# Dropping rows past a capacity: the pass-through copy cut into 4 KB pieces on one queue, with hand-written semaphores and one branch

## Chip, cores and metric

The kernel runs on one core of one Trainium2 chip. The metric is the time of one execution in device microseconds. The kernel before takes 106.83 us, the median of three runs (107.74, 106.81, 106.83).

## What is computed

`x` is float32 of shape 16 x 1024 x 512 (16,384 rows of 2 KB, 33.55 MB), `token_positions` one integer per row, `capacity` the number 256.

```python
mask = token_positions < capacity
return (x * mask[..., np.newaxis]).astype(np.float32)
```

The positions are drawn from 0 to 255, so with this input no row is dropped, and the output is a copy of `x`. Both kernels still look at every position, and both have a path for dropped rows that multiplies by the mask. That path is not taken here.

## The kernel before

Both kernels begin by copying all of `x` to the output, from device memory to device memory, before the mask is known. Meanwhile the mask is computed, and a flag tells whether any row of a section is dropped. Only where the flag is 1 is the section loaded to on-chip memory, multiplied and stored again.

**The copy (lines 73 to 77).** The 16,384 rows are seen as 128 groups ("p") of 128 rows ("n"). Copy k of four takes rows 32k to 32k+31 of every group: 128 pieces of 64 KB, one every 256 KB. Copies 0 and 2 are issued on SP's DMA queue (`hw[0]`), copies 1 and 3 on ACT's. The outermost dimension has 128 entries, and the transfer is spread over the core's 16 DMA engines in blocks of 8 entries, so that one engine's pieces begin 2 MB from the next engine's.

**The mask (lines 55 to 134).** SP first loads the positions (128 KB, line 57) into 16 partitions of 2,048 32-bit words. VectorE (DVE) converts the low and high words (L81, L82), makes four comparisons (L86 to L98) and joins them (L101 to L103). TensorE turns the 16 x 1024 result into 128 x 128 with eight selection matrices (L107), which GpSimd (POOL) has built (L60 to L65). DVE copies and sums it (L115, L118), TensorE adds the sums over partitions (L124), and DVE makes four flags of them (L126, L134). POOL also clears two 8 MB tiles (L153).

**The path for dropped rows (lines 136 to 197).** SP, ACT and DVE read four flags each. Four loads (L163) and four stores (L183) are conditional transfers: they are issued always, and move nothing where the flag is 0. The multiplications stand in an `If` on DVE. The order of waits is made by the framework: each store waits, among other things, for the copy of the same rows to have landed. SP and ACT thus stand at L183 until the copies are done.

Of the kernel before, what the change touches and what calls it, by code (L numbers as in the profile page):

```python
# [8 lines left out]
@with_exitstack  # L9
def kernel(  # L10
    ctx: ExitStack,
    tc: tile.TileContext,
    x: bass.AP,
    token_positions: bass.AP,
    capacity: bass.AP,
    out: bass.AP,
):
    nc = tc.nc
    P = nc.NUM_PARTITIONS
    fp32 = mybir.dt.float32  # L20
    i32 = mybir.dt.int32

    x_f = x.flatten_outer_dims()
    out_f = out.flatten_outer_dims()
    N, D = x_f.shape
    assert N % P == 0
    n_per_p = N // P

    x_r = x_f.rearrange("(p n) d -> p n d", p=P)
    out_r = out_f.rearrange("(p n) d -> p n d", p=P)  # L30

    tp_f = token_positions.flatten_outer_dims()
    tp_r = tp_f.rearrange("b s -> (b s)") if len(tp_f.shape) == 2 else tp_f
    tp_i32 = tp_r.bitcast(mybir.dt.int32)
    QP = 16
    G = P // QP
    tp_pn = tp_i32.rearrange("(q w) -> q w", q=QP)

    cap = float(int(capacity))

    FIX_COLS = 32
    assert n_per_p % FIX_COLS == 0
    n_fix = n_per_p // FIX_COLS
    rows_per_fix = P * FIX_COLS

    sp = nc.sync
    act = nc.scalar
    hw = (sp, act)

    mask_pool = ctx.enter_context(tc.tile_pool(name="mask", bufs=1))  # L50
    psum_pool = ctx.enter_context(tc.tile_pool(name="psum", bufs=1, space=bass.MemoryType.PSUM))
    NBUF = 2
    io_pool = ctx.enter_context(tc.tile_pool(name="io", bufs=1))

    rows_q = N // QP
    tp_tile = mask_pool.tile([QP, rows_q * 2], i32)
    sp.dma_start(out=tp_tile, in_=tp_pn)

    e_iota = mask_pool.tile([QP, P], i32, name="e_iota")
    nc.gpsimd.iota(e_iota, pattern=[[1, P]], base=0, channel_multiplier=-G)  # L60
    e_iota_f = mask_pool.tile([QP, P], fp32, name="e_iota_f")
    nc.gpsimd.tensor_copy(out=e_iota_f, in_=e_iota)  # L62
    e_all = mask_pool.tile([QP, G, P], fp32, name="e_all")
    for b in range(G):
        nc.gpsimd.tensor_scalar(  # L65
            out=e_all[:, b, :],
            in0=e_iota_f,
            scalar1=float(b),
            scalar2=None,
            op0=mybir.AluOpType.is_equal,  # L70
        )

    for k in range(n_fix):
        c0 = k * FIX_COLS
        hw[k % 2].dma_start(
            out=out_r[:, c0 : c0 + FIX_COLS, :], in_=x_r[:, c0 : c0 + FIX_COLS, :]
        )

    lo = mask_pool.tile([QP, G, P], fp32)
    hi = mask_pool.tile([QP, G, P], fp32)  # L80
    nc.vector.tensor_copy(out=lo, in_=tp_tile[:, 0 : 2 * rows_q : 2])  # L81
    nc.vector.tensor_copy(out=hi, in_=tp_tile[:, 1 : 2 * rows_q : 2])  # L82

    f_tile = mask_pool.tile([QP, G, P], fp32)
    t_hi = mask_pool.tile([QP, G, P], fp32)
    nc.vector.tensor_scalar(  # L86
        out=t_hi, in0=hi, scalar1=0.0, scalar2=None, op0=mybir.AluOpType.is_equal
    )
    m2 = mask_pool.tile([QP, G, P], fp32)
    nc.vector.tensor_scalar(  # L90
        out=m2, in0=lo, scalar1=cap, scalar2=None, op0=mybir.AluOpType.is_lt
    )
    m3 = mask_pool.tile([QP, G, P], fp32)
    nc.vector.tensor_scalar(  # L94
        out=m3, in0=lo, scalar1=0.0, scalar2=None, op0=mybir.AluOpType.is_ge
    )
    t_neg = mask_pool.tile([QP, G, P], fp32)
    nc.vector.tensor_scalar(  # L98
        out=t_neg, in0=hi, scalar1=0.0, scalar2=None, op0=mybir.AluOpType.is_lt
    )  # L100
    nc.vector.tensor_tensor(out=f_tile, in0=t_hi, in1=m2, op=mybir.AluOpType.mult)  # L101
    nc.vector.tensor_tensor(out=f_tile, in0=f_tile, in1=m3, op=mybir.AluOpType.mult)  # L102
    nc.vector.tensor_tensor(out=f_tile, in0=f_tile, in1=t_neg, op=mybir.AluOpType.add)  # L103

    m_psum = psum_pool.tile([P, P], fp32, space=bass.MemoryType.PSUM, name="m_psum")
    for b in range(G):
        nc.tensor.matmul(  # L107
            out=m_psum,
            lhsT=e_all[:, b, :],
            rhs=f_tile[:, b, :],  # L110
            start=(b == 0),
            stop=(b == G - 1),
        )
    m_tile = mask_pool.tile([P, n_fix, FIX_COLS], fp32)
    nc.vector.tensor_copy(out=m_tile, in_=m_psum)  # L115

    red = mask_pool.tile([P, n_fix], fp32)
    nc.vector.tensor_reduce(  # L118
        out=red, in_=m_tile, axis=mybir.AxisListType.X, op=mybir.AluOpType.add
    )  # L120
    ones = mask_pool.tile([P, 1], fp32)
    nc.vector.memset(ones, 1.0)  # L122
    s_psum = psum_pool.tile([1, n_fix], fp32, space=bass.MemoryType.PSUM)
    nc.tensor.matmul(out=s_psum, lhsT=ones, rhs=red, start=True, stop=True)  # L124
    flag_f = mask_pool.tile([1, n_fix], fp32)
    nc.vector.tensor_scalar(  # L126
        out=flag_f,
        in0=s_psum,
        scalar1=float(rows_per_fix) - 0.5,
        scalar2=None,  # L130
        op0=mybir.AluOpType.is_lt,
    )
    flag_i = mask_pool.tile([1, n_fix], i32)
    nc.vector.tensor_copy(out=flag_i, in_=flag_f)  # L134

    sp_flags = [
        sp.value_load(flag_i[0:1, u : u + 1], min_val=0, max_val=1)
        for u in range(n_fix)
    ]
    act_flags = [  # L140
        act.value_load(flag_i[0:1, u : u + 1], min_val=0, max_val=1)
        for u in range(n_fix)
    ]
    ve_flags = [
        nc.vector.value_load(flag_i[0:1, u : u + 1], min_val=0, max_val=1)
        for u in range(n_fix)
    ]
    eng_flags = {sp: sp_flags, act: act_flags}

    xts = []  # L150
    for b in range(NBUF):
        zt = io_pool.tile([P, FIX_COLS, D], fp32, name=f"xt_z{b}")
        nc.gpsimd.memset(zt, 0.0)  # L153
        xts.append(zt)

    ld_eng = {0: sp, 1: sp, 2: act, 3: act}
    st_eng = {0: act, 1: sp, 2: sp, 3: act}

    def emit_load_and_mul(u):
        f0 = u * FIX_COLS  # L160
        xt = xts[u % NBUF]
        eng = ld_eng[u]
        eng.dma_start(  # L163
            out=xt,
            in_=x_r[:, f0 : f0 + FIX_COLS, :],
            cond=eng_flags[eng][u],
            cond_hint=False,
        )
        with tc.If(ve_flags[u]):
            for j in range(FIX_COLS):  # L170
                nc.vector.tensor_scalar(
                    out=xt[:, j, :],
                    in0=xt[:, j, :],
                    scalar1=m_tile[:, u, j : j + 1],
                    scalar2=None,
                    op0=mybir.AluOpType.mult,
                )

    def emit_store(u):
        f0 = u * FIX_COLS  # L180
        xt = xts[u % NBUF]
        eng = st_eng[u]
        eng.dma_start(  # L183
            out=out_r[:, f0 : f0 + FIX_COLS, :],
            in_=xt,
            cond=eng_flags[eng][u],
            cond_hint=False,
        )

    emit_load_and_mul(0)  # L190
    emit_load_and_mul(1)
    emit_store(0)
    emit_store(1)
    emit_load_and_mul(2)
    emit_load_and_mul(3)
    emit_store(2)
    emit_store(3)


# [1 line left out]
_INS = ['x', 'token_positions', 'capacity']  # L201
_OUTS = [((16, 1024, 512), 'float32')]
#: Inputs that are plain numbers.
_NUMBERS = {'capacity': 256}


# [26 lines left out]
```

## Time and profile before

| What | Value |
|---|---|
| Timed runs | 107.74, 106.81, 106.83 us |
| Span of the profiled execution, first to last instruction | 104.9 us |
| Own time of the profiled execution | not listed apart; the median is 1.9 us above the span |
| DMA moved | 33.69 MB in 609 packets |
| Busy: DVE / POOL / PE | 46.6 / 50.7 / 3.9 us |
| Last DVE instruction of the mask (L134) begins | 54.51 us |

The profile is of one execution. The page lists, for each engine, busy time and groups of instructions with their mean duration. "DMA share" is the mean busy share of the core's 16 DMA engines in a stretch, and GB/s what they moved; a copy from memory to memory counts its bytes once. A packet is counted in the slice in which it begins. "SPq" and "ACTq" are the instruction queues that issue transfers. The page's memory counter (67.24 MB read, 67.11 MB written) is twice the 33.6 MB that the packets moved, which is the sum over the copies and the conditional transfers as they are written down, moved or not.

### The profile page before, as it was taken

To read this page: it belongs to the slowest core of one execution; us is meant where nothing else is said; L and a number is where in the kernel's file an instruction comes from. 1 tells how busy PE (TensorE), PEld (TensorE's weight loads), DVE (VectorE), ACT (ScalarE), POOL (GpSimd) and SP (SyncE) were. 2 spreads that over 40 slices of the span, in tenths; PEclk is the share of its full clock that TensorE was granted. 3 is DMA by queue.
4 is the path that set the end of the run, shared out by engine and by line. 5 is a ranking of instruction groups with operands and counts; after the bars stand their busy time and mean duration, and the time that the engine had idled before them with its cause. 6 is when DMAs were issued, how large, how long until landed. Compare 5 with 4: busy or idle time off the path is not lost.

```text
span 104.9 us, 202 instructions
## 1 busy us (share of the span) xinstructions
PE 3.9 (4%) x18; PEld 3.6 (3%) x18; DVE 46.6 (44%) x14; POOL 50.7 (48%) x16
## 2 busy tenths in 40 slices
PE   0000000000000000000940000000000000000000
PEld 0000000000000000000920000000000000000000
DVE  0599999999999999998030000000000000000000
POOL 7999999999999999999600000000000000000000
DMA  9299999909999939999919999759999929999930
GB/s 375 100 375 400 400 400 375 400 25 400 400 400 375 300 125 400 400 400 375 375 50 400 400 400 403 225 175 400 400 400 375 325 100 400 400 400 375 300 125 0
DMA packets 609, 33.69 MB, mean 321 GB/s; under 512 B 80, under 2 KB 80, under 8 KB 80
## 3 DMA queue, kind: packets, MB, share of 16 engines
q1 hardware_dynamic: 320, 16.91, 48.5%
q10 hardware_dynamic: 288, 16.78, 47.4%
q14 instruction: 1, 0.01, 0.0%
HBM read 67.24 MB, written 67.11 MB: 1281 GB/s over the span
## 4 chain that ended last, share of the span: by engine, by line
DVE 44%; PE 4%; DMA 3%; issue 0%
DVE lo L81 24%; DVE m L90 14%; PE m_psum L107 4%; DMA tp_tile<-in_token_positions_dram 3%; DVE f_tile L103 1%; DVE f_tile L102 1%; DVE f_tile L101 1%; DVE m L94 1%; DVE t_neg L98 1%; DVE t_hi L86 1%; DVE hi L82 1%; DVE m_tile L115 0%; DVE red L118 0%; PE s_psum L124 0%; DVE flag_f L126 0%
## 5 line engine op out<-in xcount | busy, mean ns | idle before, releaser
L153 POOL MEMSET xt_z<- 128x16384 f32 x2 | 28.0, 14012 | 0.0
L81 DVE CAST lo<-tp_tile 16x1024 f32<-16x1024 int32 x1 | 25.1, 25121 | 2.9 <-DMA tp_tile<-in_token_positions_dram 2.9
L62 POOL CAST e_iota_f<-e_iota 16x128 f32<-16x128 int32 x1 | 14.3, 14328 | 0.0
L90 DVE TENSOR_SCALAR m<-lo 16x1024 f32<-16x1024 f32 x1 | 14.3, 14305 | 0.0
L65 POOL TENSOR_SCALAR e_all<-e_iota_f 16x128 f32<-16x128 f32 x8 | 8.1, 1023 | 0.3
L107 PE MATMUL m_psum<-f_tile,e_all 16*128 16x128 f32 x16 | 3.8, 424 | 49.6 <-DVE f_tile L103 49.6
L107 PEld LDWEIGHTS m_psum<-f_tile,e_all 16*128 16x128 f32 x16 | 3.5, 326 | 49.6 <-POOL e_all L65 49.6
L115 DVE COPY m_tile<-m_psum 128x128 f32<-128x128 f32 x1 | 0.3, 292 | 3.9 <-PE m_psum L107 3.9
L103 DVE TENSOR_TENSOR f_tile<-f_tile,t_neg 16x1024 f32<-16x1024 f32 x1 | 1.2, 1211 | 0.0
L102 DVE TENSOR_TENSOR f_tile<-f_tile,m 16x1024 f32<-16x1024 f32 x1 | 1.2, 1211 | 0.0
L101 DVE TENSOR_TENSOR f_tile<-t_hi,m 16x1024 f32<-16x1024 f32 x1 | 1.2, 1204 | 0.0
L82 DVE CAST hi<-tp_tile 16x1024 f32<-16x1024 int32 x1 | 0.8, 760 | 0.0
L86 DVE TENSOR_SCALAR t_hi<-hi 16x1024 f32<-16x1024 f32 x1 | 0.8, 759 | 0.0
L94 DVE TENSOR_SCALAR m<-lo 16x1024 f32<-16x1024 f32 x1 | 0.8, 759 | 0.0
L98 DVE TENSOR_SCALAR t_neg<-hi 16x1024 f32<-16x1024 f32 x1 | 0.8, 759 | 0.0
L122 DVE MEMSET ones<- 128x1 f32 x1 | 0.1, 59 | 0.8 <-PEq L214 0.8
L60 POOL IOTA e_iota<- 16x128 int32 x1 | 0.2, 224 | 0.4 <-POOLq L214 0.4
L118 DVE TENSOR_REDUCE red<-m_tile 128x4 f32<-128x128 f32 x1 | 0.3, 286 | 0.0
L126 DVE TENSOR_SCALAR flag_f<-s_psum 1x4 f32<-1x4 f32 x1 | 0.1, 148 | 0.3 <-PE s_psum L124 0.3
L124 PE MATMUL s_psum<-red,ones 128*1 128x4 f32 x2 | 0.2, 166 | 0.7 <-DVE red L118 0.7
L214 POOL MEMSET const-float32-0.0<- 128x1 f32 x1 | 0.1, 98 | 0.2 <-issue 0.2
L134 DVE CAST flag_i<-flag_f 1x4 int32<-1x4 f32 x1 | 0.2, 156 | 0.0
(4 smaller groups left out, 0.4 us busy)
## 6 DMA issues: line engine op xcount, KB each, us to landing
tp_tile<-in_token_positions_dram SPq DMA_DIRECT2D x1, 128.0 KB
out_dram<-in_x_dram ACTq DMA_DIRECT2D x2
out_dram<-in_x_dram SPq DMA_DIRECT2D x2
xt_z<-in_x_dram SPq DMA_DIRECT2D x2
out_dram<-xt_z ACTq DMA_DIRECT2D x2
xt_z<-in_x_dram ACTq DMA_DIRECT2D x2
out_dram<-xt_z SPq DMA_DIRECT2D x2
```

Source lines behind the costliest of these rows:

```text
L62: nc.gpsimd.tensor_copy(out=e_iota_f, in_=e_iota)
L65: nc.gpsimd.tensor_scalar(out=e_all[:, b, :], in0=e_iota_f, scalar1=float(b), scalar2=None, op0=mybir.AluOpType.is_equal,)
L81: nc.vector.tensor_copy(out=lo, in_=tp_tile[:, 0 : 2 * rows_q : 2])
L82: nc.vector.tensor_copy(out=hi, in_=tp_tile[:, 1 : 2 * rows_q : 2])
L86: nc.vector.tensor_scalar(out=t_hi, in0=hi, scalar1=0.0, scalar2=None, op0=mybir.AluOpType.is_equal)
L90: nc.vector.tensor_scalar(out=m2, in0=lo, scalar1=cap, scalar2=None, op0=mybir.AluOpType.is_lt)
L94: nc.vector.tensor_scalar(out=m3, in0=lo, scalar1=0.0, scalar2=None, op0=mybir.AluOpType.is_ge)
L101: nc.vector.tensor_tensor(out=f_tile, in0=t_hi, in1=m2, op=mybir.AluOpType.mult)
L102: nc.vector.tensor_tensor(out=f_tile, in0=f_tile, in1=m3, op=mybir.AluOpType.mult)
L103: nc.vector.tensor_tensor(out=f_tile, in0=f_tile, in1=t_neg, op=mybir.AluOpType.add)
L107: nc.tensor.matmul(out=m_psum, lhsT=e_all[:, b, :], rhs=f_tile[:, b, :], start=(b == 0), stop=(b == G - 1),)
L153: nc.gpsimd.memset(zt, 0.0)
```

## The change

The copy is written anew. It goes out as 17 transfers on SP's queue alone: two of 1 MB, then fifteen of 2 MB, in order of address. Within a transfer the outermost dimension is e = 16, one entry per DMA engine; its inner dimensions are k blocks at a step of 64 KB, and 4 KB in each. Engine e thus takes the e-th 4 KB of every 64 KB.

The positions are loaded on ACT's queue into 128 partitions of 256 words, so that the mask needs no transposition: four DVE operations on 128 x 128 elements, one sum along the row, one matmul over partitions and one comparison make a single flag. The conversions of the words, the selection matrices, the eight matmuls and POOL's two 8 MB clears are gone.

The path for dropped rows stands in one `If` on SP, ACT and DVE, with plain transfers of 4 MB in two buffers. All waits are written by hand with semaphores, inside one section which the framework does not order (`tc.tile_critical()`). SP ends by waiting for all 17 copies.

```diff
-    for k in range(n_fix):
-        c0 = k * FIX_COLS
-        hw[k % 2].dma_start(
-            out=out_r[:, c0 : c0 + FIX_COLS, :], in_=x_r[:, c0 : c0 + FIX_COLS, :]
-        )
+        def copy(eng, first, count, view, **sizes):
+            eng.dma_start(
+                out=out_b[first : first + count].rearrange(view, **sizes),
+                in_=x_b[first : first + count].rearrange(view, **sizes),
+            ).then_inc(s_copy, 16)
+        KB = 1024 // 4
+        MB = 1024 * KB
+        first = 0
+        for size in [MB, MB] + [2 * MB] * 15:
+            copy(sp, first, size, "(k e c) -> e k c", e=16, c=4 * KB)
+            first += size
+            n_copy += 1
-    sp.dma_start(out=tp_tile, in_=tp_pn)
+        act.dma_start(out=tp, in_=tp_i32.rearrange("(p w) -> p w", p=P)).then_inc(s_tp, 16)
-    nc.vector.tensor_copy(out=lo, in_=tp_tile[:, 0 : 2 * rows_q : 2])
-    nc.vector.tensor_copy(out=hi, in_=tp_tile[:, 1 : 2 * rows_q : 2])
...
+        ve.wait_ge(s_tp, 16)
+        ve.tensor_scalar(
+            out=ge, in0=lo, scalar1=0.0, scalar2=None, op0=Alu.is_ge
+        ).then_inc(s_ve, 1)
...
+        ve.tensor_scalar(
+            out=drop_i, in0=total, scalar1=float(N) - 0.5, scalar2=None, op0=Alu.is_lt
+        ).then_inc(s_ve, 1)
+        for e in (sp, act, ve):
+            e.wait_ge(s_ve, 7)
...
+        with nc.If(drop):
...
-        nc.gpsimd.memset(zt, 0.0)
-    sp_flags = [
-        sp.value_load(flag_i[0:1, u : u + 1], min_val=0, max_val=1)
-        for u in range(n_fix)
-    ]
...
-        eng.dma_start(
-            out=out_r[:, f0 : f0 + FIX_COLS, :],
-            in_=xt,
-            cond=eng_flags[eng][u],
-            cond_hint=False,
-        )
...
+        sp.wait_ge(s_copy, 16 * n_copy)
```

## The prediction

> **What bounds the kernel now.** I read the page's head and its 40 slices first, then its chain, then the windows of the DMA column, and last the waits of SP's queue.
>
> ```profile
> span 104.9 us, 202 instructions
> PE 3.9 (4%) x18; PEld 3.6 (3%) x18; DVE 46.6 (44%) x14; POOL 50.7 (48%) x16
> ...
> DVE  0599999999999999998030000000000000000000
> POOL 7999999999999999999600000000000000000000
> DMA  9299999909999939999919999759999929999930
> GB/s 375 100 375 400 400 400 375 400 25 400 400 400 375 300 125 400 400 400 375 375 50 400 400 400 403 225 175 400 400 400 375 325 100 400 400 400 375 300 125 0
> ```
>
> No compute engine works in the second half; only the DMA row goes on. Its dips look like pauses and are none. A packet is 64 KB, lasts longer than a slice (2.62 us), and is counted where it begins, so now and then a slice has no beginnings. In the packet records each engine's packets follow one another without a gap: 32 of 64 KB on each of 16 engines, the first beginning at 2.25 us and the last ending at 103.09, so 100.84 us, and 100.84 / 32 = 3.15 us each. The chain (DVE 44%, PE 4%) ends with the mask at 54.7 us, half the span: it does not carry the end. The waits of SP's queue do:
>
> ```profile
> SPq L137 <- DVE flag_i L134: 52.2, 1, 52.2
> SPq L183 <- DMA out_dram<-in_x_dram: 44.5, 2, 41.7
> ```
>
> The first wait is for the flags; the second begins after it and lasts until the copies have landed. So the copies end the kernel, and the mask has some 45 us to spare. Windows placed at the packets' own boundaries show the rate (columns: stretch, length, busy time of PE, PEld, DVE and POOL with counts, clock, DMA share, GB/s):
>
> ```profile
> 2.00:5.10 3.10, 0.00 (x0) 0.00 (x0) 1.33 (x1) 3.10 (x1) 1.00 0.98 359
> 5.10:8.00 2.90, 0.00 (x0) 0.00 (x0) 2.90 (x1) 2.90 (x1) 1.00 1.01 362
> 8.00:11.00 3.00, 0.00 (x0) 0.00 (x0) 3.00 (x1) 3.00 (x1) 1.00 0.99 350
> 11.00:14.00 3.00, 0.00 (x0) 0.00 (x0) 3.00 (x1) 3.00 (x1) 1.00 1.05 350
> 14.00:17.30 3.30, 0.00 (x0) 0.00 (x0) 3.30 (x1) 3.30 (x2) 1.00 1.03 318
> ```
> ```profile
> 2.20:11.00 8.80, 0.00 (x0) 0.00 (x0) 7.23 (x1) 8.80 (x1) 1.00 1.00 360
> 11.00:23.60 12.60, 0.00 (x0) 0.00 (x0) 12.60 (x1) 12.60 (x2) 1.00 1.02 333
> 23.60:48.80 25.20, 0.00 (x0) 0.00 (x0) 25.13 (x9) 25.12 (x7) 1.00 1.00 333
> 73.90:102.20 28.30, 0.00 (x0) 0.00 (x0) 0.00 (x0) 0.00 (x0) 1.00 1.00 333
> ```
>
> The DMA engines are always taken (share about 1.00), yet move 360 GB/s at first and 333 later, with DVE and POOL busy (23.6 to 48.8) or idle (73.9 on) alike. Compute does not slow the copy. Nor is it the speed of a DMA engine by itself: the shortest 64 KB packets last 2.42 us (27.1 GB/s per engine, 434 for 16), the mean one 3.14. What the packets wait for in the other 0.7 us is on the memory's side, shared by all; which addresses the 16 engines have in hand at one time may matter to it. That address pattern is what the change touches.
>
> **The change part by part.** The sum is made against the profiled span of 104.9 us: 2.25 head + 100.84 copy + 1.8 tail. The median lies 1.9 above it.
>
> Mask and flag. Gone are 46.6 us of DVE (L81 alone 25.1, L90 14.3), POOL's 50.7 us, and the eight matmuls at L107 (3.8). In their place come six DVE operations, none over 128 elements per partition; L118 and L115 have that size at 0.29 us, so about 1.5 us, and one matmul (L124: 0.2). The gain on the end is zero, because the copy covers both chains: the new flag should stand before 15 us, over 80 us ahead of the end. What SP does after the flag (a wait, one value, one branch) comes after its 17 issues and before its wait for the copies, under the same cover. Were the cover gone, the chain of a few us would be the price. Conditional transfers: eight instructions of 0.1 to 0.3 us on two queues, most of them at 57 to 59 us, under the copies; the last two, at 103.5, stand in the tail.
>
> Head. Before, ACT issued a copy at 0.74 and SP its positions at 0.74; the first packet of the positions (16 rows) began at 1.86, that of the copy (128 rows) at 2.25. So 112 rows more cost 0.39 us. The new first transfer is 16 x 16 = 256 rows: another 0.45 us. SP issues it about 0.1 us later, behind a section entry (a no-op and a branch). First packet at 2.25 + 0.45 + 0.1 = 2.8 us, a loss of 0.55. Ends: 0 (engines begin as soon as their own rows are there) and 1.3 (all of it twice as dear).
>
> Issue. SP's issues took 418 ns for 16 rows and 609 ns for 128, 1.7 ns per row. For 512 rows that makes 1.26 us, for 256 rows 0.83: 15 x 1.26 + 2 x 0.83 = 20.6 us for the whole copy. If all of 609 ns went by rows, 4.8 ns each, it is 2.4 us per 2 MB transfer and 8,192 x 4.8 = 39 us. A 2 MB transfer takes 5.8 to 6.3 us to move, so the queue stays ahead at either price: zero, covered by the transfer before it; the 1 MB first transfer (2.9 us) covers the second's issue too. The positions go out on ACT's queue, ahead of nothing there.
>
> One queue in place of two. Each engine now takes all its pieces from one list. At most, every one of the 16 joints between transfers waits for its last write; the trace shows 0.35 us between the last packet's semaphore write and the landing, so 16 x 0.35 = 5.6 us. At least zero: in the trace the 4-byte semaphore packets last 9 ns and the next 64 KB packet begins within 20 ns, but from the other queue. I take zero, the nearer row, and keep 5.6 for the range.
>
> 4 KB pieces. An engine now has 512 pieces where it had 32. The nearest row of small pieces is the load of the positions: 8 KB packets following one another every 307 ns, against 301 ns at 27.1 GB/s, so 6 ns each; the first ones in a row lasted 461 ns, 155 more. At 6 ns a 4 KB piece takes 151 + 6 = 157 ns, and 512 take 80 us: below the copy's time now, so the engines could run ahead of the memory, and the piece itself costs nothing. At 155 ns, unhidden each time, it is 306 ns and 157 us. I take the first, since packets in a row are the case at hand; but the row writes on-chip memory and not device memory, and the other end stays open as a rival.
>
> Rate of the memory. Bounds: 333 GB/s (nothing changes), 360 (the first three rounds, as long as all engines march in step), and above it 434 (shortest packets). The new pattern keeps the 16 engines inside one 64 KB block that moves on, where they were 2 MB apart. I take 355, between the first stretch's 360 and the 350 of the next two, as the state in which engines are close together is the nearest to it: 33.55 / 0.355 = 94.5 us. This is the term that decides, and the trace does not show the pattern.
>
> Here the Trainium skill, in "HBM Reference", section "Specifications (TRN2)", puts the bandwidth of a memory domain at about 716 GB/s. The rows above are read and written at once, 2 x 333 = 667 and 2 x 360 = 720, so this trace comes up to that figure and not past it. By it the copy's floor is an estimated 67.1 / 0.716 = 93.7 us, and the total 100.2.
>
> A rule against the change stands in "DMA: Bandwidth & Descriptors", "Latency and other measured facts": copies between memory tensors in rows of 16 KB reached 214 GB/s at best, and less at large power-of-two steps (207 at 512 KB, 164 at 2 MB). This trace, with rows of 64 KB at steps of 256 KB and 2 MB, shows 333. If shorter rows are what made those copies slow, the new one would take an estimated 33.55 / 0.214 = 157 us or more; if the steps were, it gains. No run so far tells which.
>
> Tail. The last landing is at 103.43, SP's queue is through at 103.67, the span ends at 104.9. Afterwards SP has one wait and the section's exit in place of two conditional transfers. I take the same 1.8 us, with 1.3 and 2.5 as ends.
>
> Sum: 2.8 + 94.5 + 1.8 = 99.1 us of span, and 99.1 + 1.9 = 101.0.
>
> **The rivals.**
> 1. The address pattern does not matter, and the copy runs at 333 GB/s: 2.8 + 100.8 + 1.8 + 1.9 = 107.3. For it: the rate stays at 333 through all of the later stretches, whatever the other engines do. Against: the first three rounds at 360.
> 2. Slower: each 4 KB piece has a cost that the next does not hide. It decides from 100.84 / 512 = 197 ns a piece, 46 over the 151 of the bytes. At 60 over it is 211 x 512 = 108 us, in all 114.5; at the full 155, 157 us and 163. For it: 155 ns of start-up in the first packets, and 64 KB pieces that last 0.7 us longer than their bytes. Against: the 6 ns of packets in a row, and those 64 KB packets without any loss (2.42 us).
> 3. Joints on one queue: the forecast plus up to 5.6, 106.6. For it: 0.35 us to a landing; against: 9 ns packets.
> 4. The memory has more to give once the engines stand close: 157 ns a piece, 80 us, in all 86.9; halfway from 355 GB/s 94. Against: in no stretch do 16 engines together pass 362.
>
> **How the numbers follow.** Forecast 0.55, from 97 to 104 by the ends of head, tail and rate (360 to 345). Rival 1 0.11, rival 2 0.20, rival 3 0.06, rival 4 0.08. The range of 94 to 108 takes in the forecast, rivals 1 and 3 and half of rival 4, and leaves out rival 2 and the far half of 4. About 1% is what a measurement of this kernel can tell from no change. Faster by over 1% (below 105.8): the forecast, rival 4, and most of 3, 0.68. Within 1%: most of rival 1 and some of 3, 0.11. Slower: rival 2 and a part of 1, 0.21.
>
> **What would show it.** Copy stretches of a steady 350 to 360 GB/s confirm the rate; 333 says rival 1; a share of 1.00 at under 320 says rival 2; a share well under 1.00 says joints or issue. First packets before 3 us confirm the head; the last DVE instruction should end before 15 us; SP's last wait should be for the copies, and end 1 to 2 us before the span does. The prediction is wrong if the 4 KB packets last over 197 ns.

## The result, and the profile after

The changed kernel took 110.40, 110.69, 111.21 and 112.34 us, the kernel before beside it 106.81 to 107.74. The ratio is 1.034, with a 95% interval from 1.028 to 1.040: slower by about 3.4%, outside the predicted range of 94 to 108. (The 112.34 is left out of the ratio, as a disturbed run.) The profiled execution took 110.40 us over a span of 108.6, so 1.8 us lie around it.

The head of the page of the changed kernel, with its slices:

```profile
span 108.6 us, 90 instructions
PE 0.2 (0%) x2; PEld 0.1 (0%) x2; DVE 1.6 (1%) x7; POOL 0.2 (0%) x4
...
DVE  0500000000000000000000000000000000000000
DMA  2999999999999999999999999999998999999870
GB/s 71 338 305 273 389 305 339 299 299 380 279 383 264 345 327 278 342 320 330 344 312 329 276 385 288 330 338 309 353 294 326 344 344 329 302 356 312 339 308 24
DMA packets 8609, 33.69 MB, mean 310 GB/s; under 512 B 288, under 2 KB 416, under 8 KB 8608
```

The compute engines are all but gone, as the change set out: 46.6 us of DVE became 1.6, and the flag is there at 4.9 us. The DMA row shows no gap. Its rate now swings between 264 and 389 from slice to slice; with packets of 4 KB this is no artefact of counting.

The queue of SP, then the windows of the copy (columns as before):

```profile
SPq L151 <- DMA out_dram<-in_x_dram: 26.5, 1, 26.5
```
```profile
0.90 0.36 ACTq L85 DMA_DIRECT2D tp<-in_token_positions_dram  x1
0.95 79.03 SPq L69 DMA_DIRECT2D out_dram<-in_x_dram  x17
2.95 0.23 DVE L92 TENSOR_SCALAR ge<-tp 128x128 f32<-128x128 int32 x1 [1.88 <-DMA tp<-in_token_positions_dram]
```
```profile
2.50:15.10 12.60, 0.19 (x2) 0.09 (x2) 1.53 (x6) 0.00 (x0) 1.00 1.01 324
15.10:27.70 12.60, 0.00 (x0) 0.00 (x0) 0.00 (x0) 0.00 (x0) 1.00 1.03 323
27.70:52.90 25.20, 0.00 (x0) 0.00 (x0) 0.00 (x0) 0.00 (x0) 1.00 1.00 322
78.10:103.30 25.20, 0.00 (x0) 0.00 (x0) 0.00 (x0) 0.00 (x0) 1.00 0.99 329
103.30:107.00 3.70, 0.00 (x0) 0.00 (x0) 0.00 (x0) 0.00 (x0) 1.00 0.59 234
```

The wait for the copies still ends the kernel. The engines are as fully taken as before (about 1.00), at 322 to 329 GB/s, where the kernel before kept 333. In the last window the share falls to 0.59: some engines are done while others go on. By the packet records the copy begins at 2.48 us and ends at 106.95, 104.47 us against 100.84. So the whole loss (3.7 us of span) lies in the copy stretch (3.63); head and tail changed by +0.23 and -0.15 and cancel.

The packet records say more. The median 4 KB packet lasts 159 ns, the next one beginning 155 ns after it; the mean is 201. Nearly four fifths of the pieces (78%) last 165 ns or less, so they go at the engine's own speed; 9% last 300 to 1,835 ns. So an engine runs at full speed, then stands.

The 4-byte packets that end each transfer on its 16 engines show how far the engines part. In the kernel before, those of the copies lie within 0.6 to 1.0 us of one another. In the changed kernel they lie 1.0 us apart after the first transfer, 5.8 at most, and 2.5 at the last.

### The profile page after: what moved, and what is told of

Same layout as the page of the kernel before. It is cut to its first block, busy times and chain, and to the rows that moved or that the text cites. A ratio compares the mean times of both kernels' runs of the same rounds, so it can differ in the third digit from the quotient of the medians.

```text
span 108.6 us, 90 instructions
## 1 busy us (share of the span) xinstructions
PE 0.2 (0%) x2; PEld 0.1 (0%) x2; DVE 1.6 (1%) x7; POOL 0.2 (0%) x4
```

## The experiments

Two theories stood against one another at first. "Piece": each 4 KB piece has a cost that the next does not hide. "Queue": one queue, with its joints and its long issue, costs what a second would hide. A third, "closeness", was that 16 engines inside one 64 KB block collide. The chips of the runs differ by up to 2%, so only ratios to the kernel before on the same chip are compared. The packet records name neither the engine nor the address; distances between engines are those that the program writes down, with the entries of the outermost dimension taken to go to the 16 engines in order.

**1. The old copy in the new kernel.**

```diff
-        for size in [MB, MB] + [2 * MB] * 15:
-            copy(sp, first, size, "(k e c) -> e k c", e=16, c=4 * KB)
+        for k in range(4):
+            c0 = 32 * k
+            (sp, act)[k % 2].dma_start(
+                out=out_r[:, c0 : c0 + 32, :], in_=x_r[:, c0 : c0 + 32, :]
+            ).then_inc(s_copy, 16)
```

> The changed kernel with the copy of before: four transfers of 128 pieces of 64 KB on two queues. Everything else (mask, semaphores, branch) stays changed. If the loss lies in the copy alone, this takes 106 to 107 us, a copy stretch of some 100.8 us. If hand-written waits, section entry or exit cost something, it stays above 108.

It took 1.031 (1.026 to 1.037), and not for a reason that the theories named. Its timeline:

```profile
0.91 1.26 ACTq L79 DMA_DIRECT2D out_dram<-in_x_dram  x2
2.20 0.60 ACTq L85 DMA_DIRECT2D tp<-in_token_positions_dram  x1
106.98 0.23 DVE L92 TENSOR_SCALAR ge<-tp 128x128 f32<-128x128 int32 x1 [105.91 <-DMA tp<-in_token_positions_dram]
108.79 0.15 DVE L114 TENSOR_SCALAR drop_i<-total 1x1 int32<-1x1 f32 x1 [0.28 <-PE total L112]
```

The edit put ACT's two copies ahead of the positions in the same queue, so the positions landed with the copies, at 106.9 us, and the mask came after everything. The cover that the prediction relied on was gone, and the chain of a few us was the price. The edit was at fault, and the run says nothing of the copy.

**5. The same with the positions issued first** (the line of L85 moved above the loop).

> As the run with the old copy, but the positions are issued on ACT's queue ahead of ACT's two copies, so that they do not stand behind 16 MB. If the loss of the changed kernel lies in the copy's piece size alone, this ties with the kernel before (ratio 0.995 to 1.005). If section entry, exit or hand-written waits cost something, 1.01 or more.

Measured: 1.002 (0.999 to 1.005). Mask, hand-written waits, section and branch cost nothing and bring nothing that can be measured. The change's loss is the copy's.

**2 to 4. One property of the copy at a time.** Run 2 puts `c=64 * KB` for `c=4 * KB`; run 4 puts `(sp, act)[n_copy % 2]` for `sp`; run 3 moves the engines apart:

```diff
+        x_v = x_b.rearrange("(e k t c) -> t e k c", e=16, t=16, c=4 * KB)
+        out_v = out_b.rearrange("(e k t c) -> t e k c", e=16, t=16, c=4 * KB)
+        for t, k0, k1 in [(0, 0, 16), (0, 16, 32)] + [(t, 0, 32) for t in range(1, 16)]:
+            sp.dma_start(out=out_v[t][:, k0:k1, :], in_=x_v[t][:, k0:k1, :]).then_inc(s_copy, 16)
```

> The changed kernel with 64 KB in place of 4 KB: engine e takes the e-th 64 KB of every 1 MB, still 17 transfers on one queue. Theory 'piece' (each 4 KB piece has a cost of its own): 106 to 107 us, packets of 3.1 us. Theory 'closeness' (16 engines within one 64 KB block collide in memory): also near 107, since they now stand 64 KB apart. Theory 'one queue': stays at 110 to 111.

> The changed kernel with 4 KB pieces at steps of 64 KB as before, but each engine in its own 2 MB section: 2 MB apart, not 4 KB. Sizes and number of transfers, queue and pieces per engine are those of the changed kernel. Theory 'piece': 110 to 111 us again, mean piece 201 ns. Theory 'closeness': 106 to 107 us, mean piece near 195 ns. Theory 'one queue': 110 to 111.

> The changed kernel with the 17 transfers issued alternately on SP's and ACT's queues; pieces and addresses unchanged. Theory 'one queue' (joints and issue stalls that a second queue would hide): 106 to 108 us. Theories 'piece' and 'closeness': 110 to 111 us.

Measured: 64 KB pieces 1.001 (0.997 to 1.004); engines 2 MB apart 1.031 (1.025 to 1.036); two queues 1.031 (1.024 to 1.038). "Queue" and "closeness" fall: one queue with 17 transfers is as fast as the kernel before once its pieces are 64 KB, and neither a second queue nor distance helps small ones. So far "piece" stands.

**6, 8, 9, 10. Is it a fixed cost per piece?** Run 6 gives the kernel before 4 KB pieces in its four transfers on two queues. Runs 8, 9 and 10 are the changed kernel with `c=2 * KB`, `c=16 * KB` and `c=32 * KB`.

```diff
-        hw[k % 2].dma_start(
-            out=out_r[:, c0 : c0 + FIX_COLS, :], in_=x_r[:, c0 : c0 + FIX_COLS, :]
-        )
+        hw[k % 2].dma_start(out=out_b[k], in_=x_b[k])
```

(Here `out_b` and `x_b` are the tensors as `"(t k e c) -> t e k c"` with t = 4, e = 16, c = 4 KB.)

> The kernel before with one edit: its four transfers of 8 MB on two queues go by 4 KB pieces, engine e taking the e-th 4 KB of every 64 KB. Mask, conditional transfers and framework waits unchanged. Theory 'piece': ratio 1.03 against the kernel before, like the changed kernel. Theory 'the rest of the change': 1.00.

> The changed kernel with 2 KB pieces (the e-th 2 KB of every 32 KB). Theory 'a fixed cost for each piece': 3% of the time at 512 pieces per engine become 6% at 1,024, ratio 1.055 to 1.065, and the shortest 2 KB packet follows the last after about 80 ns (75.6 for its bytes and some 4). Theory 'a threshold between 4 and 64 KB': the same 1.03.

> The changed kernel with 16 KB pieces (the e-th 16 KB of every 256 KB). Theory 'a fixed cost for each piece': 128 pieces per engine, a quarter of 3%, ratio 1.005 to 1.01. Theory 'a threshold': 1.00 or 1.03.

> The changed kernel with 32 KB pieces (the e-th 32 KB of every 512 KB). So far 2, 4 and 16 KB gave 1.040, 1.031 to 1.034 and 1.037, and 64 KB 1.000, so no cost proportional to the number of pieces. Theory 'drift' (with 64 KB the engines stay in step, within 1.1 to 1.5 us at the end of each transfer, with smaller pieces they part by 2 to 6 us): a spread between, ratio 1.01 to 1.03. Theory 'size of the piece itself': 1.003, since the cost of a piece would be shared by 256 pieces less.

| Piece | Ratio to the kernel before | 95% interval | Engines apart at the last transfer's end, us |
|---|---|---|---|
| 2 KB | 1.040 | 1.036 to 1.044 | 5.8 |
| 4 KB (the changed kernel) | 1.034 | 1.028 to 1.040 | 2.5 |
| 4 KB in the kernel before | 1.022 | 1.014 to 1.030 | 4.6 |
| 16 KB | 1.037 | 1.034 to 1.039 | 2.5 |
| 32 KB | 1.028 | 1.024 to 1.032 | 2.1 |
| 64 KB | 1.001 | 0.997 to 1.004 | 0.9 |

A fixed cost per piece would have given 16 KB a quarter of the loss at 4 KB, and 2 KB twice as much. It did neither. All sizes under 64 KB cost 2 to 4%, and in all of these runs the engines end further apart than with 64 KB. That the two go together is no proof of cause: run 4, with engines 1.3 to 2.4 us apart through most of the copy, lost as much as run 3 with 3 to 5. In the profiled execution of run 18 (below) the engines of 4 KB pieces stay 1.0 to 1.8 us apart, no further than the 64 KB pieces of run 15 (1.1 to 1.8), and it lost more than runs 3 and 4.

Two other rivals fall by the same runs. The step that run 2 widened along with the piece is not what helped: at a step of 256 KB, 64 KB pieces tie (run 5) and 16 KB pieces lose 3.7% (run 9). Nor is it that SP stands while it issues: in run 10 each of the 17 issues lasted 0.57 to 0.71 us, as in run 2 (0.56 to 0.70), and run 10 still lost 2.8%.

**12 and 13. What a packet waits for.** Both leave out the path for dropped rows. They load half of x into on-chip memory, store it, and then copy the other half from memory to memory, each stretch after the last one has ended, with 64 KB and with 4 KB pieces.

```diff
+        for b in range(2):
+            sp.dma_start(out=xts[b], in_=x_r[:, 32 * b : 32 * b + 32, :]).then_inc(s_ld[0], 16)
+        sp.wait_ge(s_ld[0], 32)
+        for b in range(2):
+            sp.dma_start(out=out_r[:, 32 * b : 32 * b + 32, :], in_=xts[b]).then_inc(s_st[0], 16)
+        sp.wait_ge(s_st[0], 32)
```

> Leaves out the path for dropped rows and takes the copy apart, in three stretches after one another: half of x loaded to on-chip memory in 64 KB pieces, the same half stored, then the other half copied from memory to memory as in the kernel before. Theory 'the memory is what a packet waits for, since it is read and written at once': load and store run at 400 GB/s or more each (packets near 2.4 to 2.6 us), the copy at 325 to 335. Theory 'a 64 KB piece has 0.7 us of its own': all three at 333. Time some 155 to 165 us against 182 if all ran at 333 GB/s (3 x 16.8 MB / 333 = 151 plus waits between).

> As the three stretches before (the path for dropped rows left out), with 4 KB pieces in each. If small pieces cost an engine time whatever the memory does, load and store are 3% slower than with 64 KB; if the loss comes of reading and writing memory at once, load and store keep their 64 KB rate (less 4 ns a piece, 2.7%) and only the copy is slower.

Windows over load, store and copy, of 64 KB first and of 4 KB second:

```profile
2.40:41.00 38.60, 0.19 (x2) 0.09 (x2) 1.53 (x6) 0.00 (x0) 1.00 1.01 435
44.00:82.40 38.40, 0.00 (x0) 0.00 (x0) 0.00 (x0) 0.00 (x0) 1.00 0.95 410
84.00:135.50 51.50, 0.00 (x0) 0.00 (x0) 0.00 (x0) 0.00 (x0) 1.00 1.00 326
```
```profile
2.15:43.50 41.35, 0.19 (x2) 0.09 (x2) 1.53 (x6) 0.00 (x0) 1.00 1.02 407
45.90:86.30 40.40, 0.00 (x0) 0.00 (x0) 0.00 (x0) 0.00 (x0) 1.00 1.02 405
89.00:142.50 53.50, 0.00 (x0) 0.00 (x0) 0.00 (x0) 0.00 (x0) 1.00 0.99 313
```

Alone, a load or a store of 64 KB pieces keeps the engine at its own speed: packets of 2.43 us on average, the shortest 2.42. (The 410 counts packets by their beginnings; from first to last the store takes 38.9 us for 16.8 MB, 431 GB/s.) Only where memory is read and written at once do they last 3.21 us. So the 0.7 us that a packet loses in the copy comes with reading and writing the same memory at once, and is no cost of a packet by itself. Whether it is the mixing or the doubled traffic (2 x 321 GB/s against 431) is open; no run copied with fewer engines.

With 4 KB pieces, load and store each take longer too: 41.7 and 41.6 us against 39.8 and 38.9, so 5 and 7%, or 7 and 10 ns more a piece, with hardly anything else going on in memory. Run 13 issues 32 transfers in each of these stretches where run 12 has 2, but most of the loss sits in the pieces: the median one follows the last after some 158 and 160 ns, against 151 for its bytes. In the copy the loss is 53.9 against 52.3 us, 3%. So in a load or a store the piece has a cost of its own. That the memory's waits in a copy do not hide it fits these 3%, but is not shown apart. Each of the two kernels ran once. (Run 12 took 139.8 us in all, under the 155 to 165 expected; the expected rates themselves add up to some 135 us and the waits between.)

**11, 14 to 17. Where small pieces lie.** Run 11 takes every other 4 KB of an engine's 256 KB, then the rest. Runs 14, 16 and 17 were to let each engine go through its section in order, even pieces on SP's queue and odd ones on ACT's, with sections of 2 MB (14 and 16) or 256 KB (17). Run 15 has 64 KB pieces in sections of 256 KB.

```diff
+        view = "(e g k t c) -> g t e k c"
+        x_v = x_b.rearrange(view, g=8, e=16, t=2, c=4 * KB)
+        out_v = out_b.rearrange(view, g=8, e=16, t=2, c=4 * KB)
+        for g in range(8):
+            for t in range(2):
+                (sp, act)[t].dma_start(out=out_v[g, t], in_=x_v[g, t]).then_inc(s_copy, 16)
```

> The changed kernel with 4 KB pieces at a step of 8 KB, each engine in a section of its own, 256 KB from the next: an even pass over a 4 MB region, then an odd one. Theory 'jumps' (an engine that jumps 64 KB or more after each small piece makes memory slow): ratio 1.00 to 1.01. Theory 'piece or drift': 1.03 again, whatever the step.

> 4 KB pieces, but each engine passes through its own 2 MB in order: SP's queue issues the even 4 KB, ACT's the odd ones, so that an engine that takes turns between its two queues goes on from 4 KB to the next. Engines 2 MB apart as in the kernel before. Theory 'the piece's own 4 ns and the drift of engines': ratio 1.02 to 1.035, as with other 4 KB patterns. Theory 'jumps in address': 1.00.

> The same with 16 KB pieces, in order within the engine's 2 MB. Theory 'the piece's own 4 ns': 1.005. Theory 'address pattern' (what made 16 KB pieces at steps of 256 KB slow is where they lie): 1.00 to 1.01. If pieces under 64 KB are slow wherever they lie: 1.03 or more.

> 64 KB pieces on SP's queue alone, each engine in a section of 256 KB, 16 sections in a 4 MB region: the distance between engines of the run that took 1.27 times as long with 4 KB pieces at a step of 8 KB. Theory 'distance of 256 KB' (engines that march in step that far apart meet in the same part of memory): 1.1 or more. Theory 'half-used steps': 1.00.

> The 4 KB pieces in order through two queues, engines 256 KB apart. Theory 'distance of 256 KB': 1.1 to 1.27. Theory 'half-used steps' (the even pass by itself uses half of something that both passes together use whole): 1.03.

Measured: run 11 1.271 (1.264 to 1.277); run 14 2.263 (2.245 to 2.282); run 16 1.587 (1.575 to 1.600); run 15 1.001 (0.998 to 1.004); run 17 1.301 (1.294 to 1.309). A window of run 14:

```profile
52.00:102.00 50.00, 0.00 (x0) 0.00 (x0) 0.00 (x0) 0.00 (x0) 1.00 0.91 142
```

The engines are taken nine tenths of the time and move 142 GB/s. No theory of mine foresaw this. Nor did these three runs test order: ACT's first piece begins 4.6 to 5.4 us after SP's, and by the packet records SP's queue stays ahead, by some 16 pieces of 4 KB for each engine in runs 14 and 17 and some 4 of 16 KB in run 16. At these steps that is about 128 KB, so an engine that serves both queues by turns goes to and fro between two places in place of going on to the next piece. What pieces really in order would cost is not shown. Neither distance is bad by itself, as 64 KB pieces run at full rate with engines 64 KB (run 2), 256 KB (run 15) and 2 MB apart (run 5). It takes small pieces and a certain arrangement together.

**18 and 19. An engine's pieces made to change their place.** Pieces of 4 KB at a step of 68 KB, and of 16 KB at a step of 80 KB, engines 2 MB apart, one queue.

```diff
+        x_v = x_b.rearrange("(e k c) -> e k c", e=16, c=4 * KB)
+        out_v = out_b.rearrange("(e k c) -> e k c", e=16, c=4 * KB)
+        for t in range(17):
+            sp.dma_start(out=out_v[:, t::17, :], in_=x_v[:, t::17, :]).then_inc(s_copy, 16)
```

> 4 KB pieces, engines 2 MB apart as in the run at 1.0305, on one queue in 17 transfers, with the step between an engine's pieces 68 KB in place of 64: the place of its pieces within 64 KB moves on by 4 KB each time, where it stayed the same all through a transfer. Theory 'fixed place' (a piece under 64 KB at a step of a power of two always falls into the same part of the memory, a 64 KB piece passes through all of it): ratio 1.015 to 1.025, the piece's own 4 ns (2%) being left. Theory 'size of the piece or drift': 1.03. Theory 'small jumps are what hurts': 1.03 too, as 68 KB is no smaller than 64.

> 16 KB pieces, engines 2 MB apart, one queue, step 80 KB in place of the 256 KB of the run at 1.037. Theory 'fixed place': 1.005 to 1.01, as only a quarter of the pieces' own time is left. Theory 'any piece under 64 KB': 1.03 or more.

Run 18 took 113.4 to 119.1 us, at best 1.055 (1.051 to 1.059); run 19 took 130.6 to 143.5, too scattered for an interval, against 107.1 to 107.8 before. Run 18 is worse than run 3, which differs from it in the step and in how the pieces are dealt to the 17 transfers (1.031), so "fixed place" falls for 4 KB. Run 19 is worse than run 9 (1.037), but there the engines were 16 KB apart and not 2 MB, so it does not tell step from distance.

## Why the prediction was wrong, point by point

- **Bound: right.** The copies end the kernel before and after, and the engines have no gap. That the 0.7 us a packet loses is on the memory's side was argued from the mean and the shortest packet; run 12 shows that it comes with reading and writing the memory at once (2.43 us a packet alone, 3.21 in the copy).
- **Mask, flag, conditional transfers at zero: right.** Run 5 is within 0.5% of the kernel before, and run 1 shows the price when the cover is gone: the last DVE instruction begins at 108.79 of 111.2 us.
- **Head: right, a little too dear.** First packet at 2.48, not 2.8 (before: 2.25). **Tail:** 1.66 against 1.8.
- **Issue: the cost was wrong, the zero right.** SP's 17 issues lasted 79 us, not 20.6. But the price by rows was too dear: the first three, of 256, 256 and 512 pieces, took 0.58 to 0.70 us each, and the 17 of run 2, with 64 KB pieces, 0.56 to 0.70. Later ones took up to 13.7 us, while the median 2 MB transfer landed 30 us after its issue. So SP stands there behind work already queued, and nothing starves.
- **One queue at zero: right.** Run 2 is at 1.001 with one queue and 17 joints; run 4 at 1.031 with two queues. Rival 3 falls.
- **"The piece itself costs nothing": the step that failed first.** The 6 ns were read well (a piece follows the last after 155 ns, against 151 for its bytes). The error was to hide them, since 512 x 157 ns = 80 us is less than the copy takes. What the runs show in its place: with the rest of the changed kernel as it is, 4 KB pieces cost 3.4% and 64 KB pieces nothing (run 2, 1.001), and the copy stretch is 3.63 us longer than before. Hiding would hold if the memory set a steady pace that slower engines merely wait less for. The trace after shows bursts: nearly four fifths of the pieces go at the engine's speed, and the rest of the time is standing. If what an engine loses while it runs is added to the standing, that is 512 x 4 ns for 4 KB, about 2 us of the 3.6. Another 1.2 would come from the end: the last engine ends 1.65 us after the median one, against 0.4 before. These two add up to nearly the whole for this kernel; that is a sum that fits, and no run shows the two parts by themselves.
- **"Rate of the memory, 355 GB/s": the step that set the size.** The term was 94.5 us and measured 104.5 (321 GB/s). The 360 of the first three rounds was taken for what engines standing close together get. Runs 3, 5 and 2 give no rate that goes with closeness, and in no run did a whole copy pass 333. So of the 10 us between 94.5 and 104.5, 6.3 are a gain that closeness did not bring (94.5 to 100.8), and 3.6 the loss with small pieces. By the bandwidth in the Trainium skill's "HBM Reference", section "Specifications (TRN2)", the prediction estimated a floor of 93.7 us; the whole copy stays above it (104.5), and that a floor is near does not mean that a pattern reaches it. By its own rows the kernel before stood at 2 x 362 = 724 GB/s for 2.9 us, at that figure of about 716 or a little past it, where the prediction has it "not past it".
- **Rivals.** Rival 2 was the case: the mean piece of 201 ns lies just over its turning point of 197. As a fixed cost per piece, however, which it was, it does not hold at other sizes (table above). Its sign, a share of 1.00 at under 320 GB/s, was just missed: the windows stand at 322 to 329. The Trainium skill's rule held against the change ("DMA: Bandwidth & Descriptors", "Latency and other measured facts", 16 KB rows at 214 GB/s) had the sign right. The estimate of 157 us from it was far off for this layout (104.5), and 16 KB pieces at a step of 256 KB reached 316 GB/s here (run 9) in place of 214. Other layouts of small pieces come there: the 16 KB pieces on two queues (run 16) took a copy stretch of 165 us.
- **Range of the forecast: added up wrongly.** The ends that the prediction gives for head, tail and rate make 98.7 to 105.2, not 97 to 104. The result lies outside both.

**What stays open.** The account of 2 + 1.2 us carries over to some runs only. Against run 5 on the same chip (a copy stretch of 101.1 us in the profiled execution), it gives some 6 us for 2 KB pieces, which lost 5.7 (run 8); some 3 us for 4 KB in the kernel before, which lost 1.8 (run 6); and some 1.5 us for 16 KB pieces, which lost 5.2 (run 9, 106.3). For 16 KB most of the loss is therefore more standing. Why pieces under 64 KB make the engines stand more, from 2% to 126% with their arrangement, is not settled: distance between engines, one queue, SP's standing, jumps of 64 KB and more, and a fixed place were each taken away, and none accounts for it. Order was not taken away in the end. That engines held in step would be faster was not tried, as waits between transfers would add a cost of their own. No variant beat the kernel before; 64 KB pieces tie with it.

## What to carry to other kernels

A full DMA share says that the engines are taken, and not whether a resource paces them steadily or they run and stand by turns; look at the median packet beside the mean before hiding an engine's cost behind "the memory is slower anyway". Cut copies from memory to memory into 64 KB pieces: here they held their rate at three distances between engines and on one queue or two, while smaller pieces lost 2 to 4% in good layouts and up to 126% in bad ones; why is open. A small load that others wait for must be issued ahead of large copies in its queue: behind 16 MB it landed at 107 us in place of 3.

## What the runs showed of the hardware that was not expected

- Loads and stores of 64 KB pieces ran at 422 and 431 GB/s from first to last packet, a copy within memory at 321 to 333. A 64 KB packet lasted 2.43 us alone and 3.21 where the memory was read and written at once.
- Through a copy of 100 us with nothing to bind them, 16 engines with 64 KB pieces on one queue stayed within 0.9 to 1.8 us of one another (runs 2 and 15); with 4 KB pieces they parted by up to 5.8 us in the changed kernel, and by 1.0 to 1.8 in run 18.
- 4 KB pieces at a step of 8 KB on two queues, one queue some 128 KB ahead of the other in each engine's section, moved 138 GB/s over the whole copy with engines 2 MB apart (run 14) and 248 with 256 KB (run 17); on one queue at steps of 64 KB, with the same 2 MB between engines, 316 (run 3).
